# Eighteen seven-product units in the FFN's down projection, with their weight sums made ahead and kept in HBM

## The chip, the core and the metric

The kernel runs on one core of one Trainium2 chip. The metric is the device time of one execution in microseconds (us). Five engines with their own instruction streams share the work: TensorE (PE in the profile, its weight loads PEld), VectorE (DVE), ScalarE (ACT), GpSimd (POOL) and SyncE (SP). SP only starts DMA transfers, and POOL mostly does so here. Each engine takes its instructions in order and waits at the first one whose inputs or buffer are not ready.

## What is computed

One layer of a decoder trunk in float32: 256 tokens, D = 2048, feed-forward width 5632. The part that matters is the feed-forward network (FFN) behind the mixer, which has the two attention branches (MLA, 16 heads; a sliding window), their gates and `w_out`:

```python
def conv_ffn(h, w_up, conv_w, conv_b, w_down):
    a, b = jnp.split(h @ w_up, 2, axis=-1)
    ap = jnp.pad(a, ((0, 0), (CONV_WIDTH - 1, 0), (0, 0)))
    c = conv_b
    for j in range(CONV_WIDTH):
        c = c + conv_w[j] * ap[:, j:j + S]
    return (jax.nn.gelu(c, approximate=True) * b) @ w_down

def reference(...):
    for l in range(DEPTH):
        h = rms_norm(x, norm_mix_pre[l])
        y = hybrid_mixer(h, ...)
        x = x + rms_norm(y, norm_mix_post[l])
        h = rms_norm(x, norm_ffn_pre[l])
        y = conv_ffn(h, ffn_w_up[l], ffn_conv_w[l], ffn_conv_b[l], ffn_w_down[l])
        x = x + rms_norm(y, norm_ffn_post[l])
    return x
```

Each weight is read from HBM once; with everything else the profile counts 277.79 MB read.

## The kernel before

**A product in three passes.** Every float32 operand is split into a high part `hi` and a rest `lo`. A product of two tiles is hi·hi + hi·lo + lo·hi (`mm3`, L174–177): three 128x128 by 128x512 matmuls, at L175, L176 and L177. The split of a weight tile is `convert` (L133–145): ScalarE copies the raw tile into `whi` (L143), VectorE subtracts it from the raw tile into `wlo` (L144). A raw tile is 128 x 1024 floats, 512 KB, loaded by the SP queue (`wchunk`, or `raw_row` at L147–152). There is a ring of three raw tiles and a ring of four hi/lo pairs; a "flex" place makes it five raws or five pairs, by the stage.

**Down projection.** `w_down` has 44 rows of tiles (k = 0 to 43, each 128 x 2048). FFN columns come in eleven groups c of four k each: `ffn_up` (L1185–1222) makes up and gate columns, `conv_cols` (L1077–1092) does the convolution, the GELU and the gate product on 128x256 tiles, and the result stands as hi/lo tiles for the down projection. After c = 0 to 5 follows **down A**: k = 0 to 23 for all 2048 output columns, as two column pairs p = 0, 1 of 1024 each. After c = 6 to 10 follows the rest: **down B** for k = 24 to 43 and columns 0 to 1023, then plain products (`down`, j = 2, 3) for columns 1024 to 2047.

**Units.** `pair_gemm` (L205) works on two rows of k at a time, so on a 2 x 2 block product: two token halves, two k, two column halves. A plain unit, "p" in the order strings, takes 8 tile products, 24 matmuls. A seven-product unit, "s", gets by with 7 (21 matmuls) by a scheme of Strassen's kind. It needs sums of the activation tiles (`token_sums`, L278–288: `g_sums` and `b_sums`, made on VectorE during the up projection) and sums of the weight tiles. `seven` (L224–250) makes the latter on the spot: POOL's queue loads the two rows as `even` and `odd` (L227, L228), VectorE makes two tiles of sums `ta`, `tb` with four 128x512 subtracts (L232–235), and `odd`, half of `even`, `ta` and `tb` are converted: 3.5 raw tiles against a plain unit's two. The orders are `PAIR_ORDER = ("psppsppsppsp", "ppsppsppsppp")` for down A (4 + 3 units "s") and `B_ORDER = "pppsppspsp"` for down B (3): 10 units "s" and 24 "p".

**What sets the order.** `tick()` counts steps (one per weight tile of k in a product), and `at(t, f)` hangs work on step t: each `tick` emits what hangs on it. A scheduler then sorts what was written, engine by engine. The MLA units (attention of 16 heads) hang on steps of the products of the gates and of the sliding-window branch's output (`out_b`, `gate_b`), so that they run between their matmuls.

Of the kernel before, what the change touches and what calls it, by code (L numbers as in the profile page):

```python
# [11 lines left out]
F32 = mybir.dt.float32  # L12
# [25 lines left out]
SC_MLA = (128 + 64) ** -0.5  # L38
GELU_C = math.sqrt(2.0 / math.pi)


def trunk_layer(ctx, tc, x, x_cols_in, conv_cols_in, g_mix_post, g_ffn_post, w_in, w_q, w_kv,
# [103 lines left out]

    def raw_row(src):  # L147
        i = cnt[0]
        cnt[0] += 1
        raw = ring_tile("raw", f"raw{i}", F32, in_turn("raw"))  # L150
        nc.sync.dma_start(raw, src)
        return raw
# [51 lines left out]

    def pair_gemm(name, w, k0, c0, order, act_of, s_of, kind, d, place, sums):  # L205

        c11, c12, c21, c22 = c = banks(kind, f"c{name}_")
        q, used = [], set()
        row = lambda k: w[(k0 + k) * P:(k0 + k + 1) * P, c0:c0 + 1024]
        half = lambda w_, i: tuple(x[:, i * 512:(i + 1) * 512] for x in w_)  # L210

        def mul(o, x, w_, last=False):
            mm3(o, *x, *w_, id(o) not in used, last)
            used.add(id(o))

        def plain(u, last):
            for k in (2 * u, 2 * u + 1):
# [4 lines left out]
                tick()  # L222

        def seven(u, last):  # L224
# [5 lines left out]
            lo_, hi_ = slice(0, 512), slice(512, 1024)  # L230
            w_ = convert(odd, 1024)
            vec.tensor_tensor(ta[:, lo_], even[:, hi_], even[:, lo_], op=ALU.subtract)  # L232
            vec.tensor_tensor(ta[:, hi_], odd[:, hi_], even[:, hi_], op=ALU.subtract)
            vec.tensor_tensor(tb[:, lo_], odd[:, hi_], ta[:, lo_], op=ALU.subtract)
            vec.tensor_tensor(tb[:, hi_], odd[:, lo_], tb[:, lo_], op=ALU.subtract)
# [12 lines left out]
            mul(q6, s2, half(w_, 0), last)  # L248
            mul(c21, act_of(2 * u + 1, 1), half(w_, 1))
            tick()  # L250
            if last:
                d0, d1, d2, d3 = d() if callable(d) else d

                def first_sums():
                    act.copy(d0, q1)
                    vec.tensor_tensor(d1, d0, q6, op=ALU.add)
                    vec.tensor_tensor(d2, d1, q7, op=ALU.add)

                def more_sums():
                    vec.tensor_tensor(d3, d2, q5, op=ALU.add)  # L260
                    vec.tensor_tensor(d1, d1, q5, op=ALU.add)

                at(now[0], first_sums)
                at(now[0] + 1, more_sums)

        n = order.count("s")
        plain_of, seven_of = iter(range(n, len(order))), iter(range(n))
        for i, kd_ in enumerate(order):
            if kd_ == "s":
                u = next(seven_of)  # L270
                seven(u, u == n - 1)
            else:
                plain(next(plain_of), i == len(order) - 1)
        return c
# [464 lines left out]
    out_b(0, tb[0], (pss, "s"))  # L739
    tb[1], tb[2] = gate_pair(1)  # L740
    esg.close()

# [143 lines left out]

    b = now[0] + 26
    for u in range(8):
# [3 lines left out]

    for j in range(1, 4):
        out_b(j, tb[j], (pss, "s") if j == 1 else None)
        if j == 1:
            tb[3] = gate_b(3)
    at_ = [slot("b", p) for p in range(8)]
# [180 lines left out]
    def conv_cols(k, a, b, slot):  # L1078
# [6 lines left out]
        vec.scalar_tensor_tensor(cc[:, 2:256], a[:, 0:254], w0, cc[:, 2:256], op0=ALU.mult, op1=ALU.add)  # L1085
        act.activation(uu, cc, AF.Square)
        vec.tensor_scalar(uu, uu, 0.044715, 1.0, op0=ALU.mult, op1=ALU.add)
        vec.tensor_tensor(uu, uu, cc, op=ALU.mult)
        act.activation(uu, uu, AF.Tanh, scale=GELU_C)
# [78 lines left out]
    s_tiles = []  # L1168

    def g_sums(u):  # L1170

        if u % 2 == 0:
            s_tiles.append(sb(p3, [P, D], f"s_{u // 2}", F32R, tag=f"x2_{u // 2}"))
# [44 lines left out]

    es7 = ffn_up0()
    for c in range(1, 6):  # L1220
        if c == 2:
            for i in range(8):
                at(now[0] + i, lambda i=i: park(i // 4, i % 4))
        if c == 4:
            for u in range(4):
                at(now[0] + 3 + 3 * u, lambda u=u: g_sums(u))
        ffn_up(c, 4 * c)

# [4 lines left out]

    sevens_done = [0]

    def down_place():
        sevens_done[0] += 1
        i = sevens_done[0]
        if i % 2:
            both = sb(p6, [P, D], f"rr{i}", tag="gp")  # L1240
            return both[:, 0:1024], both[:, 1024:2048]
        return [sb(p6, [P, 1024], f"rr{i}{n}", tag="f" + n, bufs=2) for n in "ab"]

    def f_sums():
        return [sb(p6, [P, 1024], f"t{n}{cnt[0]}", tag="f" + n, bufs=2) for n in "ab"]

    for p in range(2):
        d = [dsum[t][2 * p + j] for t in range(NT) for j in range(2)]
        c = pair_gemm(f"d{p}", w_down, 0, 1024 * p, PAIR_ORDER[p], lambda k, t: (GH(k)[:, t * P:(t + 1) * P], GL(k)[:, t * P:(t + 1) * P]),
                      lambda u: s_of[u], p, d, down_place, f_sums)  # L1250
        for n_, (o, x_) in enumerate(zip(d, c)):
            at(now[0] + n_, lambda o=o, x_=x_: vec.tensor_tensor(o, o, x_, op=ALU.add))
    gpost2 = sb(p6, [P, D], "gpost2", tag="gp")
    pool.dma_start(gpost2, g_ffn_post.partition_broadcast(P))
    sb_tiles = []
    sb_of = {}

    def b_sums(u):

        if u % 2 == 0:  # L1260
            sb_tiles.append(sb(p3, [P, D], f"sb_{u // 2}", F32R, tag=f"x2_{u // 2}"))
        hi, lo = (sb_tiles[u // 2][:, (u % 2) * 1024 + i * 512:(u % 2) * 1024 + (i + 1) * 512] for i in range(2))
        a, m = (sb(s_pool[0], [P, 512], f"sb{n}{u}", tag="hx", bufs=2) for n in "am")
        sb_of[u] = token_sums(gtiles[u].bitcast(F32), a, m, hi, lo)

    for c in range(6, 11):
        if c == 9:
            for u in range(B_ORDER.count("s")):
                at(now[0] + 10 + 4 * u, lambda u=u: b_sums(u))
        ffn_up(c, 4 * (c - 6))  # L1270
# [3 lines left out]
    def z_block(acc, b, t):  # L1274
# [6 lines left out]
        act.activation(jt[:, :n], z, AF.Square, accum_out=ssz[t][:, b:b + 1])  # L1281
        vec.tensor_tensor(zo, z, gpost2[:, c0:c0 + n], op=ALU.mult)

# [24 lines left out]

    b_done = [0]

    def a_tiles(i, *n):
        return [sb(base, [P, 1024], f"dt{i}_{k}", tag=f"ahl{k}") for k in n]

    def b_place():
        b_done[0] += 1
        return a_tiles(b_done[0], *((0, 1) if b_done[0] % 2 else (4, 5)))

    ud = []

    def ud_tiles():  # L1320
        ud[:] = [x_[:, j * 512:(j + 1) * 512] for x_ in a_tiles(9, 4, 5) for j in range(2)]
# [7 lines left out]
    c_db = pair_gemm("db", w_down, 24, 0, B_ORDER, lambda k, t: (GH(k)[:, t * P:(t + 1) * P], GL(k)[:, t * P:(t + 1) * P]),  # L1329
                     lambda u: sb_of[u], 0, ud_tiles, b_place, lambda: a_tiles(20 + b_done[0], *((2, 3) if b_done[0] % 2 else (6, 7))))  # L1330
    for i in range(4):
# [110 lines left out]
```

## Time and profile before

| what | us |
|---|---|
| median of three runs | 1466.92 (1466.32 to 1467.46) |
| the profiled execution, its own time | 1466.82 |
| its span in the profile | 1464.7 |

From the trace, the stages that the change touches, by their first and last matmul:

| stage | us from the span's start |
|---|---|
| `out_b(1)`, `gate_b(3)`, `out_b(2)` begin | 283.8 |
| first MLA unit | 357.1 |
| FFN group c = 0, its second half | 754.8 to 776.4 |
| c = 1 | 776.4 to 822.9 |
| c = 2 to 5 | 822.9 to 1000.9 |
| down A, both column pairs | 1000.9 to 1126.8 |
| c = 6 to 10 | 1126.8 to 1349.4 |
| down B, columns 0 to 1023 | 1349.4 to 1402.3 |
| down, j = 2 and 3 | 1402.3 to 1456.9 |

The profile is read like this. A row of groups names line, engine, operation, output and inputs, shapes and count; behind it the busy time in all, the mean in ns of one, and the engine's idle time ahead of them with what ended it. The windows view gives one row per stretch: its length, then for each engine busy time and number of instructions, then the granted TensorE clock (1.00 is full speed), the busy share of the 16 DMA engines and the rate in GB/s. The waits view gives, per engine, line and releaser, the sum in us, the count and the longest.

### The profile page before, as it was taken

To read this page: it belongs to the slowest core of one execution; us is meant where nothing else is said; L and a number is where in the kernel's file an instruction comes from. 1 tells how busy PE (TensorE), PEld (TensorE's weight loads), DVE (VectorE), ACT (ScalarE), POOL (GpSimd) and SP (SyncE) were. 2 spreads that over 40 slices of the span, in tenths; PEclk is the share of its full clock that TensorE was granted. 3 is DMA by queue.
4 is the path that set the end of the run, shared out by engine and by line. 5 is a ranking of instruction groups with operands and counts; after the bars stand their busy time and mean duration, and the time that the engine had idled before them with its cause. 6 is when DMAs were issued, how large, how long until landed. Compare 5 with 4: busy or idle time off the path is not lost.

```text
span 1464.7 us, 20974 instructions
## 1 busy us (share of the span) xinstructions
PE 1454.3 (99%) x7567; PEld 1242.8 (85%) x7567; DVE 1088.9 (74%) x1925; ACT 837.7 (57%) x1382; POOL 70.2 (5%) x123
## 2 busy tenths in 40 slices
PE   9999999999999999999999999999999999999997
PEld 7888888888888888888888888888888888888886
DVE  7788896645667665768799976778786687677776
ACT  7588874544555554445666655555454565565553
POOL 0012110000000001000000000000000000000000
PEclk9999999999999999999999999999999999999999
DMA  8755376477655559755766666665656666667573
GB/s 296 216 164 168 105 261 197 160 212 199 188 159 159 165 162 337 263 186 173 235 206 179 199 188 187 191 187 185 206 192 207 201 186 191 186 196 232 163 234 136
DMA packets 147605, 287.60 MB, mean 196 GB/s; under 512 B 18428, under 2 KB 29597, under 8 KB 147373
## 3 DMA queue, kind: packets, MB, share of 16 engines
q1 hardware_dynamic: 137824, 252.60, 56.2%
q0 software_dynamic: 9584, 33.61, 7.3%
q8 instruction: 59, 0.97, 0.3%
q14 instruction: 46, 0.37, 0.1%
q10 hardware_dynamic: 92, 0.05, 0.0%
HBM read 277.79 MB, written 8.44 MB: 195 GB/s over the span
## 4 chain that ended last, share of the span: by engine, by line
PE 94%; DVE 2%; issue 2%; ACT 1%; DMA 1%; POOL 0%; DVEq 0%; ACTq 0%; POOLq 0%
PE accg L175 12%; PE accg L177 12%; PE accg L176 12%; PE ua L1185 10%; PE ub L1185 10%; PE ua L1189 5%; PE ub L1189 5%; PE cd L177 2%; PE cd L175 2%; PE cd L176 2%; PE mpo L875 1%; PE cg L175 1%; PE cw L177 1%; PE cg L177 1%; PE cw L176 1%
## 5 line engine op out<-in xcount | busy, mean ns | idle before, releaser
L144 DVE TENSOR_TENSOR wlo<-raw,whi 128x1024 fp32r<-128x1024 f32 (+2 forms) x470 | 568.4, 1214 | 248.2 <-ACT whi L143 241.2
L143 ACT CAST whi<-raw 128x1024 fp32r<-128x1024 f32 (+2 forms) x470 | 487.9, 1043 | 405.0 <-PE accg L177 156.9
L175 PE MATMUL accg<-whi,ahl 128*128 128x512 f32 (+1 forms) x416 | 162.8, 391 | 0.0
L177 PE MATMUL accg<-whi,ahl 128*128 128x512 f32 (+1 forms) x416 | 160.6, 386 | 0.0
L176 PE MATMUL accg<-wlo,ahl 128*128 128x512 f32 (+1 forms) x416 | 159.8, 384 | 0.0
L1185 PE MATMUL ub<-ahl,whi 128*128 128x512 f32 x640 | 154.6, 391 | 0.0
L1185 PE MATMUL ua<-ahl,whi 128*128 128x512 f32 x640 | 154.6, 391 | 0.0
L175 PE MATMUL accg<-whi,bhl 128*128 128x512 f32 x378 | 148.1, 392 | 0.0
L177 PE MATMUL accg<-whi,bhl 128*128 128x512 f32 x378 | 147.4, 390 | 0.0
L176 PE MATMUL accg<-wlo,bhl 128*128 128x512 f32 x378 | 147.3, 390 | 0.0
L1185 PEld LDWEIGHTS ub<-ahl,whi 128*128 128x128 f32 x640 | 117.5, 188 | 22.9 <-ACT cc L1083 0.3
L1185 PEld LDWEIGHTS ua<-ahl,whi 128*128 128x128 f32 x640 | 117.5, 188 | 22.7
L177 PEld LDWEIGHTS accg<-whi,ahl 128*128 128x128 f32 x416 | 78.1, 188 | 15.4
L176 PEld LDWEIGHTS accg<-wlo,ahl 128*128 128x128 f32 x416 | 78.2, 188 | 13.1
L175 PEld LDWEIGHTS accg<-whi,ahl 128*128 128x128 f32 x416 | 78.2, 188 | 13.0
L1189 PEld LDWEIGHTS ub<-ahl,wlo 128*128 128x128 f32 x640 | 82.2, 191 | 3.2
L1189 PEld LDWEIGHTS ua<-ahl,wlo 128*128 128x128 f32 x640 | 82.2, 191 | 3.1
L1189 PE MATMUL ua<-ahl,wlo 128*128 128x256 f32 x640 | 83.7, 283 | 0.0
L177 PEld LDWEIGHTS accg<-whi,bhl 128*128 128x128 f32 x378 | 71.0, 188 | 14.8
L175 PEld LDWEIGHTS accg<-whi,bhl 128*128 128x128 f32 x378 | 71.0, 188 | 14.4
L1189 PE MATMUL ub<-ahl,wlo 128*128 128x256 f32 x640 | 83.2, 283 | 0.0
L176 PEld LDWEIGHTS accg<-wlo,bhl 128*128 128x128 f32 x378 | 71.0, 188 | 14.3
(616 smaller groups left out, 2376.7 us busy)
## 6 DMA issues: line engine op xcount, KB each, us to landing
raw<-in_ffn_w_up_dram SPq DMA_DIRECT2D x176, 512.0 KB, 4.5
raw<-in_w_in_dram SPq DMA_DIRECT2D x105, 512.0 KB, 4.5
raw<-in_ffn_w_down_dram SPq DMA_DIRECT2D x68, 512.0 KB, 4.6
raw<-in_w_o_swa_dram SPq DMA_DIRECT2D x32, 512.0 KB, 4.0
raw<-in_w_o_mla_dram SPq DMA_DIRECT2D x32, 512.0 KB, 5.4
raw<-in_w_out_dram SPq DMA_DIRECT2D x26, 512.0 KB, 4.5
bias<-strip POOLq DMA_DIRECT2D x16, 256.0 KB, 4.3
raw<-in_mla_w_q_up_dram SPq DMA_DIRECT2D x32, 128.0 KB, 2.5
```

What stands on the lines that cost most here:

```text
L143: act.copy(hi[:, a:b], raw[:, a:b])
L144: vec.tensor_tensor(lo[:, a:b], raw[:, a:b], hi[:, a:b].bitcast(F32), op=ALU.subtract)
L175: pe.matmul(o, ah, bh, start=start, stop=False)
L176: pe.matmul(o, ah, bl, start=False, stop=False)
L177: pe.matmul(o, al, bh, start=False, stop=stop)
L875: pe.matmul(o, w(t), p_[:, c], start=n == 0, stop=n == 5)
L1185: pe.matmul(acc[i], hi[:, c], hn[p][:, j * 512:(j + 1) * 512], start=p + j == 0, stop=stop)
L1189: pe.matmul(acc[i][:, 0:256], lo[:, c], hn[p][:, j * 512:j * 512 + 256], start=False, stop=False)
```

## The change

- Eight more units become seven-product units: `PAIR_ORDER` has 6 + 6 "s" and `B_ORDER` 6. That is 18 "s" and 16 "p".
- The weight sums of all 18 are made ahead. `park_sums` hangs on steps of other stages: POOL loads the two rows (1 MB) into a staging tile, VectorE makes the four 128x512 subtracts in place (`less`, tied in written order by `keep_in_program_order`), POOL writes the two tiles of sums to HBM. Four are made during `out_b(1)`, `gate_b(3)` and `out_b(2)` (five steps apart), eight in c = 1 to 4 (seven or eight steps apart), six in c = 6 to 8 (eight steps apart).
- `seven_parked` takes the place of `seven`: SP's queue loads the odd row, half of the even row and the two tiles of sums, 3.5 raw tiles, and each is converted. No subtracts are left there.
- In down A and down B the ring of raw tiles is seven deep: the three, and tiles that are free in these stages (`fa`, `fb`; in B the halves of `ahl`, which hold the up projection's activations until c = 10 ends). In down A the flex place goes from raws to hi/lo pairs at step 8.
- Token sums are made for 6 units (used by both pairs) and 6, before 4 and 3.
- The GELU's polynomial folds 0.044715 into the scale of the Square: one VectorE instruction in place of two, for 44 column tiles.
- `out_b(1)`, `gate_b(3)` and `out_b(2)` are written ahead of the MLA units, which begin two steps after them; the matmuls come out in the order of before. The norm's gain `gpost2` is loaded into other tiles before down B.

```diff
+    def park_sums(name, w, k, c0, pl, tag, t0, bufs=None):
+
+        td = [dram.tile([P, 1024], F32, name=f"{name}{i}") for i in range(2)]
+        st = []
+
+        def load():
+            st.append(sb(pl, [P, D], f"{name}s", tag=tag, bufs=bufs))
+            for i in range(2):
+                pool.dma_start(st[0][:, i * 1024:(i + 1) * 1024], w[(k + i) * P:(k + i + 1) * P, c0:c0 + 1024])
+
+        def less(o, x, y):
+            o, x, y = (st[0][:, i * 512:(i + 1) * 512] for i in (o, x, y))
+            tc.keep_in_program_order(vec.tensor_tensor(o, x, y, op=ALU.subtract))
+
+        def even():
+            less(0, 1, 0)
+            less(1, 3, 1)
+            pool.dma_start(td[0], st[0][:, 0:1024])
+
+        def odd():
+            less(3, 3, 0)
+            less(2, 2, 3)
+            pool.dma_start(td[1], st[0][:, 1024:2048])
+
+        at(t0 - 5, load)
+        at(t0, even)
+        at(t0 + 1, odd)
+        return td
...
+        def seven_parked(u, last):
+            s1, s2, s3, s4 = s_of(u)
...
+            w_ = convert(raw_row(row(2 * u + 1)), 1024)
+            mul(c11, act_of(2 * u + 1, 0), half(w_, 0))
+            mul(c12, s4, half(w_, 1))
+            w_ = convert(raw_row(row(2 * u)[:, 0:512], 512), 512)
+            mul(q1, act_of(2 * u, 0), half(w_, 0), last)
+            w_ = convert(raw_row(parked[u][0]), 1024)
+            mul(q5, s1, half(w_, 0), last)
+            mul(q7, s3, half(w_, 1), last)
+            tick()
+            w_ = convert(raw_row(parked[u][1]), 1024)
+            mul(q6, s2, half(w_, 1), last)
+            mul(c21, act_of(2 * u + 1, 1), half(w_, 0))
+            tick()
...
+    parked_a = [park_a(i, pg, "gr", now[0] + 5 + 5 * i, bufs=2) for i in range(EARLY)]
+    out_b(1, tb[1], (pss, "s"))
+    tb[3] = gate_b(3)
+    out_b(2, tb[2])
...
-    b = now[0] + 26
+    b = now[0] + 2
...
-        act.activation(uu, cc, AF.Square)
-        vec.tensor_scalar(uu, uu, 0.044715, 1.0, op0=ALU.mult, op1=ALU.add)
-        vec.tensor_tensor(uu, uu, cc, op=ALU.mult)
+        act.activation(uu, cc, AF.Square, scale=GELU_R)
+        vec.scalar_tensor_tensor(uu, uu, 1.0, cc, op0=ALU.add, op1=ALU.mult)
...
+    for i in range(2 * NA - EARLY):
+        parked_a.append(park_a(i + EARLY, p6, "gp", now[0] + 8 + 15 * i // 2))
...
+    f_raw = lambda n: lambda name: sb(p6, [P, 1024], name, tag="f" + n, bufs=2)
+
+    def deep_raws():
+        turn_flex("w")
+        more_raw[:] = [raw_of, f_raw("a"), raw_of, f_raw("b"), raw_of, f_raw("a"), f_raw("b")]
+
+    turn_flex("raw")
+    at(now[0] + 8, deep_raws)
...
+    parked_b = [park_sums(f"tb{i}_", w_down, 24 + 2 * i, 0, p6, "gp", now[0] + 6 + 8 * i) for i in range(NB_)]
...
+    a_raw = lambda k: lambda name: a_tile(name, k)
+    more_raw[:] = [raw_of, a_raw(2), raw_of, a_raw(3), raw_of, a_raw(6), a_raw(7)]
...
-B_ORDER = "pppsppspsp"
+B_ORDER = "psspsspssp"
-PAIR_ORDER = ("psppsppsppsp", "ppsppsppsppp")
+PAIR_ORDER = ("ppspspsspssp", "ppspspsspssp")
+EARLY = 4
```

Three places show how instructions move. The first is VectorE in down A, around one "s" unit of the second column pair (`rr` is its pair of raw rows, loaded by POOL; `ta`, `tb` the sums). Before:

```order
L232 TENSOR_TENSOR ta746_10892<-rr7_10889 128x512
L233 TENSOR_TENSOR ta746_10892<-rr7_10889 128x512
L234 TENSOR_TENSOR tb746_10893<-rr7_10889,ta746_10892 128x512
L144 TENSOR_TENSOR wlo736_10798<-ta734_10774,whi736_10797 128x1024
L235 TENSOR_TENSOR tb746_10893<-rr7_10889,tb746_10893 128x512
L144 TENSOR_TENSOR wlo737_10808<-tb734_10775,whi737_10807 128x1024
L144 TENSOR_TENSOR wlo739_10820<-raw738_10817,whi739_10819 128x1024
L144 TENSOR_TENSOR wlo741_10838<-raw740_10835,whi741_10837 128x1024
```

After, the last two "s" units and the "p" behind them, in the same stage:

```order
L145 TENSOR_TENSOR wlo791_11082<-raw790_11079,whi791_11081 128x1024
L145 TENSOR_TENSOR wlo793_11094<-raw792_11091,whi793_11093 128x512
L145 TENSOR_TENSOR wlo795_11103<-raw794_11100,whi795_11102 128x1024
L145 TENSOR_TENSOR wlo797_11115<-raw796_11112,whi797_11114 128x1024
L145 TENSOR_TENSOR wlo799_11127<-raw798_11124,whi799_11126 128x1024
L145 TENSOR_TENSOR wlo801_11139<-raw800_11136,whi801_11138 128x512
L145 TENSOR_TENSOR wlo803_11148<-raw802_11145,whi803_11147 128x1024
L145 TENSOR_TENSOR wlo805_11160<-raw804_11157,whi805_11159 128x1024
L145 TENSOR_TENSOR wlo807_11172<-raw806_11169,whi807_11171 128x1024
L145 TENSOR_TENSOR wlo809_11193<-raw808_11190,whi809_11192 128x1024
```

The subtracts are gone from the stage, and "s" units stand back to back.

The second place is VectorE in c = 2, among the conversions of up-projection weights and the GELU of that group (`uu`, `cc`). Before:

```order
L144 TENSOR_TENSOR wlo567_8651<-raw566_8648,whi567_8650 128x1024
L1090 SCALAR_TENSOR_TENSOR uu8_8750<-uu8_8750,cc8_8749 128x256
L1087 TENSOR_SCALAR uu9_8807<-uu9_8807 128x256
L1087 TENSOR_SCALAR uu10_8864<-uu10_8864 128x256
L1088 TENSOR_TENSOR uu9_8807<-uu9_8807,cc9_8806 128x256
L144 TENSOR_TENSOR wlo569_8673<-raw568_8670,whi569_8672 128x1024
```

After (`ta7_s` is the staging tile of one pair of rows):

```order
L145 TENSOR_TENSOR wlo567_8733<-raw566_8730,whi567_8732 128x1024
L233 TENSOR_TENSOR ta7_s_8639<-ta7_s_8639 128x512
L145 TENSOR_TENSOR wlo569_8758<-raw568_8755,whi569_8757 128x1024
L233 TENSOR_TENSOR ta7_s_8639<-ta7_s_8639 128x512
L1159 SCALAR_TENSOR_TENSOR uu8_8841<-uu8_8841,cc8_8840 128x256
L233 TENSOR_TENSOR ta7_s_8639<-ta7_s_8639 128x512
L1157 SCALAR_TENSOR_TENSOR uu9_8897<-uu9_8897,cc9_8896 128x256
L233 TENSOR_TENSOR ta7_s_8639<-ta7_s_8639 128x512
L1157 SCALAR_TENSOR_TENSOR uu10_8953<-uu10_8953,cc10_8952 128x256
L145 TENSOR_TENSOR wlo571_8796<-raw570_8793,whi571_8795 128x1024
```

The four subtracts of one pair of rows now stand among the conversions, and the GELU has one instruction (L1157) where it had two (L1087, L1088).

The third place is SP's queue where down B begins. Before, it loads the rows of the first three plain units (the "s" units' rows are POOL's):

```order
L131 DMA raw920_13150<-in_ffn_w_up_dram 128x2x512
L151 DMA raw922_13190<-in_ffn_w_down_dram 128x1024
L151 DMA raw924_13208<-in_ffn_w_down_dram 128x1024
L151 DMA raw926_13239<-in_ffn_w_down_dram 128x1024
L151 DMA raw928_13257<-in_ffn_w_down_dram 128x1024
L151 DMA raw930_13288<-in_ffn_w_down_dram 128x1024
L151 DMA raw932_13306<-in_ffn_w_down_dram 128x1024
```

After (`tb0_0` and `tb0_1` are the first unit's two tiles of sums, `tb1_0` and `tb1_1` the second's; the raws' numbers, as in raw970, rise in the order in which the conversions take them):

```order
L132 DMA raw968_13388<-in_ffn_w_up_dram 128x2x512
L160 DMA raw970_13432<-in_ffn_w_down_dram 128x1024
L160 DMA raw974_13484<-in_ffn_w_down_dram 128x1024
L160 DMA raw972_13450<-in_ffn_w_down_dram 128x1024
L160 DMA raw978_13505<-tb0_0_11210 128x1024
L160 DMA raw976_13496<-in_ffn_w_down_dram 128x512
L160 DMA raw984_13553<-in_ffn_w_down_dram 128x512
L160 DMA raw986_13562<-tb1_0_11212 128x1024
L160 DMA raw988_13574<-tb1_1_11213 128x1024
L160 DMA raw980_13517<-tb0_1_11211 128x1024
L160 DMA raw990_13598<-in_ffn_w_down_dram 128x1024
L160 DMA raw982_13541<-in_ffn_w_down_dram 128x1024
```

The queue now carries all rows of two "s" units at the start, and issues some ahead of others that are used sooner: `tb0_1_11211`, the first unit's second tile of sums, stands behind three tiles of the next unit.

More of the change, by code (lines that the diff above doesn't have):

```diff
@@ L39 @@
 GELU_C = math.sqrt(2.0 / math.pi)
+GELU_R = math.sqrt(0.044715)
 def trunk_layer(ctx, tc, x, x_cols_in, conv_cols_in, g_mix_post, g_ffn_post, w_in, w_q, w_kv,
@@ L145, in convert, with raw_row @@
         return hi, lo
-    def raw_row(src):
+    more_raw = []
+    raw_of = lambda name: ring_tile("raw", name, F32, False)
+    def raw_row(src, n=1024):
         i = cnt[0]
         cnt[0] += 1
-        raw = ring_tile("raw", f"raw{i}", F32, in_turn("raw"))
-        nc.sync.dma_start(raw, src)
+        if more_raw:
+            make = more_raw.pop(0)
+            more_raw.append(make)
+            raw = make(f"raw{i}")
+        else:
+            raw = ring_tile("raw", f"raw{i}", F32, in_turn("raw"))
+        nc.sync.dma_start(raw[:, :n], src)
         return raw
@@ L203, in banks, with weight_sums, park_a, pair_gemm @@
                 for i in range(4)]
-    def pair_gemm(name, w, k0, c0, order, act_of, s_of, kind, d, place, sums):
+    def weight_sums(even, odd, ta, tb):
+        a, b = slice(0, 512), slice(512, 1024)
+        vec.tensor_tensor(ta[:, a], even[:, b], even[:, a], op=ALU.subtract)
+        vec.tensor_tensor(ta[:, b], odd[:, b], even[:, b], op=ALU.subtract)
+        vec.tensor_tensor(tb[:, a], odd[:, b], ta[:, a], op=ALU.subtract)
+        vec.tensor_tensor(tb[:, b], odd[:, a], tb[:, a], op=ALU.subtract)
+    def park_sums(name, w, k, c0, pl, tag, t0, bufs=None):
[20 more added lines that the diff above has]
+        return td
+    def park_a(i, pl, tag, t0, **kw):
+        return park_sums(f"ta{i}_", w_down, 2 * (i % NA), 1024 * (i // NA), pl, tag, t0, **kw)
+    def pair_gemm(name, w, k0, c0, order, act_of, s_of, kind, d, place=None, sums=None, parked=None):
         c11, c12, c21, c22 = c = banks(kind, f"c{name}_")
@@ L222, in plain @@
                 tick()
+        def seven_parked(u, last):
+            s1, s2, s3, s4 = s_of(u)
+            if not q:
+                q[:] = banks(1 - kind, f"q{name}_")
+            q1, q5, q7, q6 = q
+            w_ = convert(raw_row(row(2 * u + 1)), 1024)
[11 more added lines that the diff above has]
+            tick()
+            if last:
+                end_sums()
         def seven(u, last):
@@ L229, in seven @@
             ta, tb = sums()
-            lo_, hi_ = slice(0, 512), slice(512, 1024)
             w_ = convert(odd, 1024)
[L232 to L235, printed above, removed]
+            weight_sums(even, odd, ta, tb)
             if not q:
@@ L251, in seven, with end_sums, first_sums, more_sums @@
             if last:
[L252 to L264, printed above, removed]
+                end_sums()
+        def end_sums():
+            q1, q5, q7, q6 = q
+            d0, d1, d2, d3 = d() if callable(d) else d
+            def first_sums():
+                act.copy(d0, q1)
+                vec.tensor_tensor(d1, d0, q6, op=ALU.add)
+                vec.tensor_tensor(d2, d1, q7, op=ALU.add)
+            def more_sums():
+                vec.tensor_tensor(d3, d2, q5, op=ALU.add)
+                vec.tensor_tensor(d1, d1, q5, op=ALU.add)
+            at(now[0], first_sums)
+            at(now[0] + 1, more_sums)
         n = order.count("s")
@@ L270, in pair_gemm @@
                 u = next(seven_of)
-                seven(u, u == n - 1)
+                (seven_parked if parked else seven)(u, u == n - 1)
             else:
@@ L891, in trunk_layer @@
         mla_unit(u, b + 4 * u)
[L893 to L896, printed above, removed]
+    out_b(3, tb[3])
     at_ = [slot("b", p) for p in range(8)]
@@ L1226, in trunk_layer @@
                 at(now[0] + 3 + 3 * u, lambda u=u: g_sums(u))
+        if c == 5:
+            for u in range(4, NA):
+                at(now[0] + 3 + 5 * (u - 4), lambda u=u: g_sums(u))
         ffn_up(c, 4 * c)
@@ L1232, in down, with turn_flex @@
         return gemm(xh, xl, w_down, k0, nk, c0, n, split=split, ps=ps)
[L1234 to L1245, printed above, removed]
+    def turn_flex(kind):
+        flex[0] = kind
+        turn.update(raw=0, w=0)
+    f_raw = lambda n: lambda name: sb(p6, [P, 1024], name, tag="f" + n, bufs=2)
[4 more added lines that the diff above has]
+    at(now[0] + 8, deep_raws)
     for p in range(2):
@@ L1264, in b_sums @@
         sb_of[u] = token_sums(gtiles[u].bitcast(F32), a, m, hi, lo)
+    parked_b = [park_sums(f"tb{i}_", w_down, 24 + 2 * i, 0, p6, "gp", now[0] + 6 + 8 * i) for i in range(NB_)]
     for c in range(6, 11):
         if c == 9:
-            for u in range(B_ORDER.count("s")):
-                at(now[0] + 10 + 4 * u, lambda u=u: b_sums(u))
+            for u in range(NB_):
+                at(now[0] + 2 + 4 * u, lambda u=u: b_sums(u))
         ffn_up(c, 4 * (c - 6))
```

32 lines of the change are left out of this document (18 added, 14 removed).

## The prediction

> **What bounds the kernel now.** I read the page first, busy times and the chain of waits, then the waits view of PE.
>
> ```profile
> span 1464.7 us, 20974 instructions
> PE 1454.3 (99%) x7567; PEld 1242.8 (85%) x7567; DVE 1088.9 (74%) x1925; ACT 837.7 (57%) x1382; POOL 70.2 (5%) x123
> ...
> PE 94%; DVE 2%; issue 2%; ACT 1%; DMA 1%; POOL 0%; DVEq 0%; ACTq 0%; POOLq 0%
> PE warm L77 <- DVE ramp L66: 1.1, 1, 1.1
> PE pstrip L349 <- DMA sel<-in_strip_sel_dram: 0.8, 1, 0.8
> PE cdb L176 <- DVE wlo L144: 0.2, 1, 0.2
> ```
>
> PE is busy 99% of the span and makes 94% of the chain that ended last. In the whole execution the view shows three PE waits, two at the start and one of 0.2 us in down B. So the time is the number of matmuls times their pitch, as long as weights arrive converted. Whether they do is asked stage by stage, with the windows view (length; busy time and count for PE, PEld, DVE, ACT, POOL; clock; DMA share; GB/s):
>
> ```profile
> 283.80:349.40 65.60, 65.60 (x291) 54.30 (x291) 34.16 (x33) 29.32 (x31) 1.10 (x2) 1.00 0.72 210
> 571.00:584.00 13.00, 13.00 (x63) 10.77 (x62) 9.26 (x15) 5.84 (x7) 1.63 (x4) 1.00 1.04 383
> 776.40:822.90 46.50, 46.50 (x274) 41.04 (x273) 42.35 (x82) 30.73 (x54) 0.00 (x0) 1.00 0.61 186
> 822.90:1000.90 178.00, 178.00 (x1025) 157.32 (x1024) 131.42 (x224) 101.36 (x163) 0.54 (x1) 1.00 0.64 190
> 1000.90:1126.80 125.90, 125.90 (x557) 104.28 (x556) 97.17 (x114) 64.20 (x73) 6.33 (x12) 1.00 0.61 196
> 1126.80:1349.40 222.60, 222.60 (x1282) 196.73 (x1281) 164.56 (x272) 124.23 (x195) 2.11 (x4) 1.00 0.67 199
> 1349.40:1402.30 52.90, 52.74 (x233) 43.38 (x232) 39.65 (x53) 27.41 (x36) 1.06 (x2) 1.00 0.55 174
> ```
>
> Down A (1000.9) runs without a gap. Seven "s" and seventeen "p" are 7 x 21 + 17 x 24 = 555 matmuls (the row has two of the neighbouring groups besides), so the pitch is 125.9 / 555 = 0.2268 us. The clock is full throughout. A step of the up projection is 222.6 / 80 = 2.78 us, one of a plain product 12 x 0.2268 = 2.72.
>
> **What it removes.** Five units in down A and three in down B turn from "p" to "s": 8 x 3 = 24 matmuls, 24 x 0.2268 = **5.44 us** off the path. No other matmul is added or goes. The whole question is what feeds them.
>
> **Conversions in the down stages.** The groups by shape give the prices:
>
> ```profile
> L144 DVE TENSOR_TENSOR wlo<-raw,whi 128x1024 fp32r<-128x1024 f32 x458 | 558.7, 1224 | 246.2 <-ACT whi L143 239.3 <-PE ub L1185 3.0 <-PE ua L1185 2.5
> L144 DVE TENSOR_TENSOR wlo<-raw,whi 128x512 fp32r<-128x512 f32 x4 | 2.6, 690 | 2.0 <-ACT whi L143 2.0
> L143 ACT CAST whi<-raw 128x1024 fp32r<-128x1024 f32 x458 | 479.8, 1052 | 402.3 <-PE accg L177 156.2 <-PE ua L1185 48.7 <-DMA raw<-in_ffn_w_down_dram 48.1
> L143 ACT CAST whi<-raw 128x512 fp32r<-128x512 f32 x4 | 2.4, 616 | 1.9 <-DMA raw<-in_w_in_dram 1.9
> L232 DVE TENSOR_TENSOR ta<-rr 128x512 f32<-128x512 f32 x4 | 2.8, 688 | 0.1
> L284 DVE TENSOR_TENSOR sm<-sa,sm 128x128 f32<-128x128 f32 x4 | 1.2, 288 | 0.1
> L1087 DVE TENSOR_SCALAR uu<-uu 128x256 f32<-128x256 f32 x44 | 12.2, 287 | 0.7 <-ACT uu L1086 0.5
> L1088 DVE TENSOR_TENSOR uu<-uu,cc 128x256 f32<-128x256 f32 x44 | 18.3, 419 | 0.3
> L1207 DVE SCALAR_TENSOR_TENSOR f<-ub,f 128x256 f32<-128x256 f32 x40 | 14.2, 417 | 10.4 <-ACT f L1206 10.4
> ```
>
> An "s" costs PE 21 x 0.2268 = 4.76 us. Before, VectorE gave it 3 x 1.224 + 0.69 = 4.36 for conversions and 4 x 0.688 = 2.75 for sums: 7.11, more than PE, so the kernel could afford few of them, with "p" (2.45 on VectorE, 5.44 on PE) between. After, the 2.75 are gone and even "ss" fits: 4.36 against 4.76 on VectorE, 3 x 1.052 + 0.616 = 3.77 on ScalarE. VectorE no longer limits these stages, and the one stall of down B, where a `wlo` came late, may go with the sums:
>
> ```profile
> 1370.46 0.39 PE L175 MATMUL cdb<-whi,bhl 128*128 128x512 f32 x1
> ...
> 1371.00 0.50 PE L176 MATMUL cdb<-wlo,bhl 128*128 128x512 f32 x1 [0.15 <-DVE wlo L144]
> ```
>
> Start to start that is 0.54 us where the pitch is 0.23, and this matmul takes 0.11 longer than the one ahead: some 0.4 us, a gain between 0 and 0.4. I take 0.4, against a loss below.
>
> **Sums that move.** 18 x 2.75 = 49.5 us of VectorE work, 27.5 of it there before, go to stages where PE sets the pace. Token sums (two at about 0.69 and four at 0.288, 2.5 us for a unit) come five times more, 12.7 us; the GELU pays it back, (0.287 + 0.419 - 0.417) x 44 = 12.7 us. By stage: in 283.8 to 349.4 VectorE is busy 34.16 of 65.6, and four parks add 11. In c = 1 it is 42.35 of 46.5, two parks add 5.5, the GELU takes off 1.2: 46.7, full. In c = 2 to 5, 131.42 + 16.5 + 5.1 - 4.6 = 148 of 178. In c = 6 to 10, 164.56 + 16.5 + 7.6 - 5.8 = 183 of 222.6. So only c = 1 is over, by 0.2 us, and there conversions run ahead. ScalarE's waits in c = 1 to 5 show it:
>
> ```profile
> ACT whi L143 <- PE ua L1185: 22.6, 17, 2.7
> ACT whi L143 <- PE ub L1185: 20.1, 19, 2.7
> ```
>
> ScalarE waited 42.7 us for PE to give back a pair, that is with every pair full, four of them at 2.78 us. This hides the sums; I cost them at nothing. Without that cover c = 1 would cost 0.2 us, and every park up to its 2.75.
>
> **Park traffic.** A park loads 1.05 MB and writes 1.05 MB. In c = 1 to 4 that is 2.1 MB in 7.5 steps (20.9 us), 100 GB/s on top of 190; in the early stage 2.1 MB in 5 steps (13.6 us), 154 on top of 210: 364 GB/s for 55 us. Both are under the 383 GB/s that the stretch at 571 shows with PE full. The load is issued five steps (13.6 us) ahead of its subtracts. If it is later, the subtract holds VectorE's queue, so the `wlo` behind it, and PE only after four pairs (11 us) more. Cost nothing; bound from above in the rivals.
>
> **Loads of the down stages.** This is the one place where the sum could turn. An "s" now moves 3.5 x 0.524 = 1.835 MB where it moved 1.05. "ss" needs 3.67 MB in 9.53 us, 385 GB/s; "ssp" 4.72 in 14.97, 315; down A and B together 18 x 1.835 + 16 x 1.049 = 49.8 MB in 762 x 0.2268 = 172.8 us, 288 GB/s, where the rows show 196 and 174. The nearest rows:
>
> ```profile
> raw<-in_ffn_w_down_dram SPq DMA_DIRECT2D x68, 512.0 KB, 4.6
> raw<-in_w_o_mla_dram SPq DMA_DIRECT2D x5, 512.0 KB, 6.9
> ACT whi L143 <- DMA raw<-in_ffn_w_down_dram: 25.2, 9, 6.3
> ```
>
> The second is from the stretch 571 to 584, the densest loading, with PE full. A place of the seven-deep ring comes back after two units, 9.5 us in "ss", less 2.3 us of conversion: 7.2 us for a landing that took 4.6 at 190 GB/s and 6.9 at 383. It fits, narrowly. The third row is down A before: ScalarE waited nine times for a load, without PE noticing. Where down B begins it is tighter. The second unit's odd row stands in SP's queue behind a place that the fourth pair of conversions gives back, so it starts some 1.7 us into B at best (0.616 + 0.69 for the half row's conversion, which begins as B does, and an estimated 0.4 until the issue); it must be there at 5.44 + 4.76 - 2.28 = 7.9. At 4.6 it is 1.6 early, at 6.9 it is 0.7 late. Bounds for each of the seven "ss" (four in A, three in B): 0 and 0.7. I take 0.5 in all, near the lower end, since six of the seven begin with a ring filled during the "p" ahead.
>
> [...]
>
> **The sum.** 1466.82 (the profiled execution) - 5.44 - 0.4 + 0.5 = 1461.5. That execution lies 0.1 below the median 1466.92, so against the median it is the same within rounding. Forecast **1461.5**, its own range 1460.6 to 1462.4.
>
> **Rivals.** *A. Loads become the bound; slower.* If the down stages get less than 49.8 MB / 178.3 us = 279 GB/s (178.3 being 786 x 0.2268, what the same units take now), the gain is gone. At 265 GB/s they take 188 us, 15 more than planned, and the kernel 1476; at 270, 1473. For it: no stage of that length ran over 210 GB/s in the rows, the landing of 6.9 us at the dense place, and tiles that must be written to HBM and read again. Against it: 383 GB/s with nothing lost on PE. *B. The "ss" come late by up to 0.7 each*, in-order loads behind places that come back late: two to seven of them in place of the 0.5, 1462.4 to 1465.9, in the middle 1464.1. For it: the start of B above. Against it: "p" units between, which need only 193 GB/s. *C. Parks hold VectorE.* One staging tile serves all parks of the FFN stages, so a load waits for the last write. Write and load at 6.9 each behind the subtracts' two steps give 5.6 + 6.9 + 6.9 = 19.4 of 20.9 us. If each of the 18 lost 0.3 us, 5.4 are gone: 1466.9, no change. Against it: eleven microseconds of pairs ahead. That the matmuls don't go is no rival: PE's own list of instructions is 24 matmuls shorter.
>
> **How the numbers follow.** Forecast 0.66, B 0.18, C 0.05, A 0.11. A measurement of this kernel can tell about 0.2%, 2.9 us, from no change: faster is below 1464.0. Faster: 0.66 + two thirds of B + a fifth of C = 0.79. Same: the rest of B and most of C, and the lightest cases of A: 0.11. Slower: 0.10. The range takes the forecast's and nearly all of B, 1460.6 to 1466.0; A and half of C are left out, and the lowest tail.
>
> **What would show it.** In the changed profile, down A (540 matmuls) should last 122.5 us and down B (222) 50.4, PE gapless, at 280 to 320 GB/s. VectorE in down A falls to 12 x 4.36 + 12 x 2.45 plus what else is there, some 90 us. C = 1 keeps its 46.5. PE waits on `wlo` or on DMA in "ss" mean B; a rate stuck below 280 with ScalarE waiting for `raw` means A; PE waits in c = 1 to 8 or in 283 to 357 mean C. The forecast is wrong if the 24 matmuls are gone and the down stages are not 5.4 us shorter, or if a stage that only took in moved work gets longer.

## The result

| kernel | median, us | lowest to highest | runs |
|---|---|---|---|
| before | 1466.46 | 1465.82 to 1467.64 | 10 |
| changed | 1469.97 | 1467.43 to 1473.88 | 10 |

The ratio of the changed kernel to the one before is 1.0025, with a 95% interval of 1.0014 to 1.0035: slower by about 3.5 us, where 1461.5 was forecast. Its runs also spread over 6.5 us, those of before over 1.8. A fixed amount of extra work would add the same time to every run, so the spread suggests that something in it is near a limit.

The page of the changed kernel, from the lines on span, busy time and the chain that ended last:

```profile
span 1470.6 us, 21276 instructions
PE 1453.6 (99%) x7543; PEld 1239.7 (84%) x7543; DVE 1119.9 (76%) x1959; ACT 850.3 (58%) x1403; POOL 98.6 (7%) x176
...
PE 75%; DVE 10%; DMA 9%; ACT 3%; issue 2%; DVEq 0%; ACTq 0%; SPq 0%
```

The 24 matmuls are gone (7543 against 7567). But PE makes 75% of the chain instead of 94%, and VectorE and DMA have come in with 10% and 9%. The waits view of PE, which had one entry of 0.2 us behind the start:

```profile
PE ub L1261 <- DVE wlo L145: 4.0, 4, 2.3
PE ua L1261 <- DVE wlo L145: 1.5, 2, 1.2
PE qd L184 <- ACT whi L144: 1.1, 1, 1.1
...
PE qd L185 <- DVE wlo L145: 0.8, 1, 0.8
PE cd L185 <- DVE wlo L145: 0.3, 1, 0.3
```

Most of it waits in `ub` and `ua`, the up projection, whose matmuls the change does not touch. The windows view places it (columns as in the prediction):

```profile
283.80:349.40 65.60, 65.60 (x291) 54.35 (x290) 44.28 (x49) 29.37 (x31) 7.51 (x14) 1.00 0.92 304
776.30:889.40 113.10, 113.10 (x657) 100.07 (x656) 98.35 (x176) 65.62 (x109) 9.61 (x18) 1.00 0.77 248
889.40:1006.40 117.00, 112.62 (x642) 98.74 (x642) 88.44 (x145) 63.44 (x104) 6.40 (x12) 1.00 0.78 251
1006.40:1133.50 127.10, 124.96 (x542) 102.27 (x541) 92.33 (x100) 74.52 (x85) 1.06 (x2) 0.99 0.82 276
1133.50:1357.80 224.30, 223.24 (x1281) 196.96 (x1280) 176.68 (x292) 126.30 (x200) 12.80 (x24) 1.00 0.78 251
1357.80:1408.30 50.50, 50.50 (x224) 41.81 (x223) 41.54 (x51) 31.75 (x40) 0.00 (x0) 1.00 0.92 321
```

| stage | before | changed | difference |
|---|---|---|---|
| c = 1 to 5 | 224.5 | 230.1 | +5.6 |
| down A | 125.9 | 127.1 | +1.2 (122.5 forecast) |
| c = 6 to 10 | 222.6 | 224.3 | +1.7 |
| down B | 52.9 | 50.5 | -2.4 (50.4 forecast) |

These add up to +6.1; the two spans differ by 5.9. Down B did what was forecast, at 321 GB/s and without a gap. The loss is in the up projection, where parks came in, and where down A starts behind it. The first park stage (283.8), where the flex place belongs to raws, runs at 304 GB/s without a gap. The second half of c = 1 to 5 loses; the first half (776.3 to 889.4) does not.

Why, ScalarE's waits in c = 1 to 5 (776.4 to 1000.9) of the changed kernel tell:

```profile
ACT whi L144 <- DMA raw<-in_ffn_w_up_dram: 53.7, 30, 6.2
```

The DMA view of the same stretch (count, size, median us from issue to landing):

```profile
raw<-in_ffn_w_up_dram SPq DMA_DIRECT2D x74, 512.0 KB, 4.8
ta<-ta_s POOLq DMA_DIRECT2D x16, 512.0 KB, 4.7
ta_s<-in_ffn_w_down_dram POOLq DMA_DIRECT2D x14, 512.0 KB, 6.6
```

Before, ScalarE waited 42.7 us there for PE to give back a pair: the converter was ahead. Now it waits 53.7 us for raw tiles: it is behind. Yet the raws' median landing only rose to 4.8 us; the same row of the kernel before:

```profile
raw<-in_ffn_w_up_dram SPq DMA_DIRECT2D x74, 512.0 KB, 4.4
```

The worst place, from the changed kernel's timeline of ScalarE (start, duration, in brackets the idle time ahead and what ended it):

```profile
942.62 1.07 ACT L144 CAST whi<-raw 128x1024 fp32r<-128x1024 f32 x1
943.56 0.62 ACT L1153 ACTIVATE cc<-f,cvT 128x256 f32<-128x256 f32 x1
950.41 1.04 ACT L144 CAST whi<-raw 128x1024 fp32r<-128x1024 f32 x1 [6.23 <-DMA raw<-in_ffn_w_up_dram]
```

And of PE:

```profile
952.77 1.22 PE L1261 MATMUL ub<-ahl,wlo 128*128 128x256 f32 x8 [2.25 <-DVE wlo L145]
```

A raw tile was issued at 940.4, behind a park's 1 MB at 939.8, and landed 9.95 us later. ScalarE stood 6.2 us, and PE ran out of pairs. In the first half of the stage ScalarE stood 22.6 us for raw tiles as well (14 times, the longest 4.2), and PE did not wait at all: there the lateness was paid out of the stock of converted pairs.

### The profile page after: what moved, and what is told of

Read it like the earlier page. It is cut to its first block, busy times and chain, and to the rows that moved or that the text cites. A ratio compares the mean times of both kernels' runs of the same rounds, so it can differ in the third digit from the quotient of the medians.

```text
span 1470.6 us, 21276 instructions
## 1 busy us (share of the span) xinstructions
PE 1453.6 (99%) x7543; PEld 1239.7 (84%) x7543; DVE 1119.9 (76%) x1959; ACT 850.3 (58%) x1403; POOL 98.6 (7%) x176
## 4 chain that ended last, share of the span: by engine, by line
PE 75%; DVE 10%; DMA 9%; ACT 3%; issue 2%; DVEq 0%; ACTq 0%; SPq 0%
PE accg L184 12%; PE accg L186 12%; PE accg L185 12%; DMA raw<-in_ffn_w_up_dram 8%; PE ua L1257 4%; DVE wlo L145 4%; PE ub L1257 3%; PE ua L1261 2%; PE cd L185 2%; PE cd L186 2%; PE cd L184 2%; ACT whi L144 2%; PE ub L1261 2%; DVE ta_s L233 1%; PE mpo L948 1%
## 5 line engine op out<-in xcount | busy, mean ns | idle before, releaser
L145 DVE TENSOR_TENSOR wlo<-raw,whi 128x1024 fp32r<-128x1024 f32 (+2 forms) x526 | 624.5, 1195 | 243.0 <-ACT whi L144 238.0
L144 ACT CAST whi<-raw 128x1024 fp32r<-128x1024 f32 (+2 forms) x526 | 537.0, 1028 | 431.0 <-PE accg L186 157.3
L1257 PEld LDWEIGHTS ub<-ahl,whi 128*128 128x128 f32 x640 | 117.5, 188 | 22.6
```

The lines of the kernel that those rows point to most:

```text
L144: act.copy(hi[:, a:b], raw[:, a:b])
L145: vec.tensor_tensor(lo[:, a:b], raw[:, a:b], hi[:, a:b].bitcast(F32), op=ALU.subtract)
L1257: pe.matmul(acc[i], hi[:, c], hn[p][:, j * 512:(j + 1) * 512], start=p + j == 0, stop=stop)
```

## The experiments

Theory 1 after this view: the parks' transfers make the raw loads of the up projection late. There are three raw tiles, so one must come round (issue, landing, 1.05 + 1.22 us of conversion) within three steps, 8.3 us; a landing above 6.0 us puts the converter behind. Theory 2, the prediction's rival C: the parks' subtracts hold VectorE's in-order queue. Theory 3: the writes to HBM do it.

### No transfers, no subtracts, no writes

Each leaves out one part of the 14 parks in the FFN stages; the four early ones stay.

```diff
 e1_no_park_dma
+            if tag == "gp" and keep.get(name[:2]):
+                st.append(keep[name[:2]])
+                return
...
-            pool.dma_start(td[0], st[0][:, 0:1024])
+            if tag != "gp":
+                pool.dma_start(td[0], st[0][:, 0:1024])
 e2_no_park_sub
-            less(0, 1, 0)
-            less(1, 3, 1)
+            if tag != "gp":
+                less(0, 1, 0)
+                less(1, 3, 1)
 e3_no_park_write
-            pool.dma_start(td[0], st[0][:, 0:1024])
+            if tag != "gp":
+                pool.dma_start(td[0], st[0][:, 0:1024])
```

> The 14 parks of the FFN stages keep their four subtracts but neither load nor write (one load each in c = 1 and c = 6 fills the tile); the down stages read plain rows of w_down of the same size in place of their sums, so the output is not the reference's. Theory 1 (the parks' transfers make the up projection's raw loads late, in a ring of three, and the pairs ahead are used up): the 5.5 us lost in c = 3 to 5 and the 1.2 in c = 8 go, down A starts with its pairs ahead, 1461 to 1463. Theory 2 (the subtracts hold VectorE's queue): nothing gained, 1468 to 1472. Theory 3 (only the writes to HBM hurt): 1461 to 1463 as well.

> The 14 parks of the FFN stages keep loads and writes but not their subtracts, so raw rows are written and the output is not the reference's. Theory 1 (transfers): little gained, 1466 to 1471. Theory 2 (subtracts in VectorE's queue): the loss goes, 1461 to 1463. Theory 3 (writes): 1466 to 1471.

> The 14 parks of the FFN stages keep loads and subtracts but write nothing; the down stages read plain rows of w_down in place of those sums, so the output is not the reference's. Theory 1 (all transfers of the parks, the 1 MB load bursts above all): some of the loss stays, 1462 to 1467. Theory 2 (subtracts): 1468 to 1472. Theory 3 (writes alone): all of the loss goes, 1461 to 1463.

| kernel | median, us | lowest to highest | ratio to before, 95% |
|---|---|---|---|
| no transfers | 1460.58 | 1459.32 to 1461.92 | 0.9957 (0.9942 to 0.9972) |
| no subtracts | 1469.50 | 1467.77 to 1473.34 | 1.0024 (1.0012 to 1.0035) |
| no writes | 1465.45 | 1460.83 to 1469.14 | 0.9990 (0.9980 to 1.0001) |

Without the transfers the whole gain stands; without the subtracts nothing is gained. That speaks against theory 2. Alone it is not quite clean: without subtracts to wait for, the writes also start sooner after the loads. The five raws below keep every subtract, and settle it. Without the writes about half comes back in the median, so theory 3 falls too, as the only cause: loads and writes both count. Where PE loses the time differs between the profiled executions: without subtracts it waited in c = 1 already (at 794.0 and 810.4 us), without writes it waited in down A and in c = 6 to 10 (226.4 us there) and not in c = 1 to 5. The windows of the kernel without transfers, c = 1 to 5 and down A:

```profile
775.20:999.80 224.60, 224.60 (x1298) 198.62 (x1297) 188.37 (x322) 131.52 (x217) 0.00 (x0) 1.00 0.64 195
999.60:1122.20 122.60, 122.60 (x542) 101.52 (x541) 91.68 (x99) 73.36 (x83) 1.07 (x2) 1.00 0.81 270
```

VectorE has all of its added work there (188 us) and PE loses nothing. Down A, which still loads as many bytes, takes 122.6 us, the 122.5 of the forecast. So its excess in the changed kernel came with the stage ahead of it.

The kernel without subtracts still shows how a late load reaches PE. From its timeline in c = 1:

```profile
781.01 1.06 POOL L229 DMA_DIRECT2D ta_s<-in_ffn_w_down_dram  x2 [5.55 <-DMA ta<-ta_s]
...
782.07 11.16 SPq L132 DMA_DIRECT2D raw<-in_ffn_w_up_dram  x4
...
790.53 1.05 ACT L144 CAST whi<-raw 128x1024 fp32r<-128x1024 f32 x1 [2.66 <-DMA raw<-in_ffn_w_up_dram]
...
791.61 1.23 DVE L145 TENSOR_TENSOR wlo<-raw,whi 128x1024 fp32r<-128x1024 f32 x1 [3.28 <-ACT whi L144]
792.75 0.42 DVE L1161 SCALAR_TENSOR_TENSOR uu<-uu,cc 128x256 f32<-128x256 f32 x1
```

POOL starts two rows at 781.0. SP's raw at 782.07 lands at 790.45, after 8.4 us. ScalarE, then VectorE, stand in front of it, and the GELU's `uu` waits behind `wlo` in VectorE's queue. PE's waits view there names `uu`, not a load (3.1 us at `fT`). Followed back, it is the load: here a raw tile that took 8.4 us reached PE through VectorE's queue, and not as a missing pair.

### Five raws in the FFN stages

```diff
     es7 = ffn_up0()
+    flex[0] = "raw"
+    turn.update(raw=0, w=0)
...
     more_raw.clear()
-    turn.update(raw=0)
+    turn_flex("raw")
...
+    turn_flex("w")
     a_raw = lambda k: lambda name: a_tile(name, k)
```

> The whole change, with the two flex places given to raw tiles from c = 1 to 5 and c = 6 to 10: five raws and four hi/lo pairs where there were three and five. Theory 1 (late loads in a ring of three): a landing of up to 5 x 2.78 - 2.3 = 11.6 us is now covered where 6.0 was, so c = 1 to 5 lose 0 to 1 us and the time is 1461 to 1465. Theory 2 (subtracts hold VectorE): one pair less of cover, so the same or worse, 1470 to 1475. Theory 3 (writes): between them, 1462 to 1467.

1461.49 us (1460.73 to 1466.03), ratio 0.9971 (0.9961 to 0.9980). No transfer was taken away; two places were only renamed from pairs to raws. The profiled execution (1464.21) has one stall left, where down A goes over to c = 6:

```profile
1128.00:1131.40 3.40, 0.93 (x5) 0.51 (x4) 0.61 (x1) 1.41 (x2) 0.00 (x0) 1.00 0.10 38
1131.40:1134.00 2.60, 2.60 (x8) 2.02 (x7) 2.50 (x3) 2.57 (x3) 0.00 (x0) 0.51 0.30 47
```

At 38 GB/s hardly anything is loading: SP's queue had stood 2.6 us in front of a flex place that still held a pair of down A (it waited for a matmul of `cd`, the view of SP's waits says). The next experiment takes those out of use four steps earlier:

```diff
     for p in range(2):
...
+        if p:
+            at(now[0] + 20, lambda: turn_flex("raw"))
```

> The kernel e4_raw5 with one stall of its profile taken away: there SP's queue, at the start of c = 6, waited for flex places that still held hi/lo pairs of down A, and PE lost 4.2 us in the profiled execution (2.6 of stall, the rest at half clock behind it). Here the flex places are no longer given to pairs in the last four steps of down A. If that transition was what spread e4's times (1460.7 to 1466.0), the median is 1460.5 to 1461.5 and the spread under 3 us. If the spread comes from elsewhere (parks of c = 6 to 8), as e4: 1461 to 1462 with a spread of 5.

**1460.08 us** (1459.75 to 1460.42), ratio 0.9955 (0.9942 to 0.9969), beside 1466.47 for the kernel before. It beats both kernels, and its five runs spread over 0.7 us. ScalarE's waits in c = 1 to 5:

```profile
ACT whi L144 <- PE ua L1257: 24.0, 18, 2.7
ACT whi L144 <- PE ub L1257: 17.3, 14, 2.7
```

The raws' landing there, in the DMA view:

```profile
raw<-in_ffn_w_up_dram SPq DMA_DIRECT2D x73, 512.0 KB, 5.1
```

And the chain that ended last, from the page:

```profile
PE 96%; DVE 2%; ACT 1%; issue 1%; DMA 0%; DVEq 0%; ACTq 0%
```

The loads land later than in the changed kernel (median 5.1 against 4.8, and 14 of 74 took more than 6 us, the longest 9.0), at 263 GB/s against 250, with every subtract in its place. Yet ScalarE waits for PE again, as before, and PE has no wait in the stage. In this kernel late loads did no harm with enough of them under way: five raws cover 11.6 us, and the longest landing was 9.0.

### Fewer raws, or only in one part

> The kernel e5_raw5_tail with one raw tile fewer in the FFN stages: four raws and four pairs. Theory 1: a ring of four covers a landing of 4 x 2.78 - 2.3 = 8.8 us, above nearly all that the profiles show beside parks (90% under 6.7), so nearly all of the gain: 1460 to 1462. If it is something else that the fifth raw brings, between e5 and the changed kernel: 1463 to 1467.

```diff
+    deep = [2]
...
-        return flex[0] == kind and turn[kind] % (RAW + 2 if kind == "raw" else RING + 1) >= (RAW if kind == "raw" else RING)
+        return flex[0] == kind and turn[kind] % (RAW + deep[0] if kind == "raw" else RING + 1) >= (RAW if kind == "raw" else RING)
...
     flex[0] = "raw"
+    deep[0] = 1
```

1459.92 us (1459.29 to 1461.99), ratio 0.9958 (0.9943 to 0.9973): the fourth raw tile brings all of it, as 4 x 2.78 - 2.3 = 8.8 us says. In its trace 16 of 74 raws took more than 6 us, none more than 7.7, and PE has no wait. (The edit is not exactly a ring of four. Three of four loads find their place four steps back; the fourth goes to the flex place, which keeps its two buffers in turn, so it can start up to a step earlier.)

> The whole change with five raws in c = 1 to 5 alone; c = 6 to 10 keep three raws and five pairs. By theory 1 c = 6 to 8, where a park comes every 22 us, lose what the changed kernel lost there, 1 to 2 us, with some spread: 1461 to 1463. If three raws are enough at that spacing: as e5, 1460 to 1460.5.

```diff
     es7 = ffn_up0()
+    flex[0] = "raw"
+    turn.update(raw=0, w=0)
```

1462.56 us (1460.79 to 1465.39), ratio 0.9974 (0.9964 to 0.9983). Against 1460.08 that is some 2.5 us, at the upper end of what was expected and with its spread. The profiled execution (1462.92) puts only half of it where three raws are: c = 6 to 10 took 223.9 us, and 222.7 with five. PE's waits behind the start:

```profile
PE x2T L1071 <- DVE x L1068: 1.3, 1, 1.3
...
PE ub L1261 <- DVE wlo L145: 0.5, 1, 0.5
```

The second lies in c = 8. The first lies at 740.9 us, ahead of the FFN, in a place that this edit does not touch; what delayed it is not known. So three raws in c = 6 to 10 cost 1.2 us in this execution; how the other runs divide is open.

> The kernel before, with the two flex places given to raws in c = 1 to 5 and back to pairs in down A and after: a control for e4. Before has no stall there, so by theory 1 five raws give nothing: 1466 to 1467. If five raws and four pairs are better in themselves, whatever the parks do, it gains as e4 did, 1462 to 1464.

```diff
     es7 = ffn_up0()
+    flex[0] = "raw"
+    turn.update(raw=0, w=0)
     for c in range(1, 6):
...
+    flex[0] = "w"
+    turn.update(raw=0, w=0)
     for p in range(2):
```

1466.20 us (1465.04 to 1466.79), ratio 0.9997 (0.9988 to 1.0006). Five raws give nothing to the kernel before: the gain is not theirs.

### Are the bursts to blame?

```diff
-            for i in range(2):
+            for i in range(2 if tag != "gp" else 1):
                 pool.dma_start(st[0][:, i * 1024:(i + 1) * 1024], ...)
...
         at(t0 - 5, load)
+        if tag == "gp":
+            at(t0 - 3, lambda: pool.dma_start(st[0][:, 1024:2048], w[(k + 1) * P:(k + 2) * P, c0:c0 + 1024]))
```

> The whole change with three raws as it is, but each park of the FFN stages loads its two rows two steps (5.6 us) apart instead of at once; the same bytes in all. If the bursts do it (a raw load queued behind 1 MB lands 8 to 10 us late in a ring that covers 6), landings stay under 7 us and the loss of 5.5 us in c = 3 to 5 falls to 0 to 2: 1462 to 1466. If the bytes as such do it (the mean rate of 250 GB/s), no change: 1468 to 1472. If VectorE's queue waits for the later second row, worse: 1470 to 1474.

1469.27 us (1466.10 to 1471.63), ratio 1.0020 (1.0011 to 1.0029): nothing gained. I had taken the 1 MB burst for the culprit; spreading it by two steps leaves the median landing at 4.8 us and the time as it was. It did not make the landings punctual either: 13 of 68 raws took more than 6 us, the longest 10.4, where the unsplit loads had 12 of 67 and 9.95. So it is the added traffic on a ring of three; that no other spacing would help is not shown.

### The GELU

> The kernel e4_raw5 with the GELU of before (two VectorE instructions for one, 12.7 us more of VectorE over c = 0 to 10). If only late loads count, nothing is lost: 1461 to 1462.5. If VectorE's queue is near its limit beside the parks' subtracts, 1463 to 1468.

```diff
-        act.activation(uu, cc, AF.Square, scale=GELU_R)
-        vec.scalar_tensor_tensor(uu, uu, 1.0, cc, op0=ALU.add, op1=ALU.mult)
+        act.activation(uu, cc, AF.Square)
+        vec.tensor_scalar(uu, uu, 0.044715, 1.0, op0=ALU.mult, op1=ALU.add)
+        vec.tensor_tensor(uu, uu, cc, op=ALU.mult)
```

1462.50 us (1460.74 to 1464.77). This did not decide: `e4_raw5` itself spread up to 1466 through its stall at c = 6. The same edit on the clean kernel:

> The kernel e5_raw5_tail with the GELU of before: 12.7 us more of VectorE, nothing else. Theory 1 (only late loads in a short ring count): 1460 to 1461. If VectorE is near its limit beside the parks' subtracts: 1462 to 1464.

1459.83 us (1459.33 to 1460.75), ratio 0.9954 (0.9937 to 0.9970): 12.7 us more of VectorE cost nothing. The folded GELU is neither cause nor help.

## Why the prediction was wrong

**The gain itself was right.** With loads in time, down A takes 122.6 us and down B 50.5 (122.5 and 50.4 forecast), and the kernel 1460.08, 6.4 under before. The forecast's 5.44 + 0.4 make 5.8 of it (the spans of the two profiled executions differ by 6.0); the remaining half microsecond was not traced. The 0.5 us that the sum held back for the "ss" was not needed.

**The dense down stages were right.** They were the feared place, at up to 385 GB/s. Seven raws under way carry them: 276 GB/s in down A, 321 in down B, no wait of PE in B. Rivals A and B did not occur: the waits in down A fall in the first "s" behind two "p", not in an "ss", and with loads in time they are gone.

**The step that failed is "Park traffic", with its cost of nothing.** It set 100 GB/s on top of 190 against the 383 that the chip had shown, found room, and stopped. The room was there (250 GB/s came). What the parks cost measured +5.6 us in c = 1 to 5, +1.7 in c = 6 to 10, and 4.6 in down A (127.1 against 122.5), 11.9 in all against a gain of 5.8. The 383 GB/s had been reached with five raws; the FFN stages have three, since the flex place belongs to pairs there. With three, rate was not the limit (with five, the same stage moves 263 GB/s without a gap), but the time for one tile to come round: 4.4 + 2.3 = 6.7 of 8.3 us before, 1.6 to spare. Of the 67 raws issued between 776.4 and 1000.9 us whose landing the changed kernel's trace gives, 12 took more than 6 us; before, 2 of 69. For the seven-deep ring of the down stages the prediction had done this very sum (7.2 us for a landing of 4.6 to 6.9); at its own 6.9 a ring of three, with room for 6.0, is too short.

**The cover was there, but it was a stock.** The "eleven microseconds of pairs ahead" were true at c = 1, and in this execution they held for the first half of the stage. But a ring with 1.6 us to spare refills slowly, and the next park came before the stock was full again: ScalarE waited for PE to give back a pair, the sign of a full stock, 3.5 us in all of c = 1 to 5, where it had waited over 42 before. PE's first wait falls at 909.8 us; from there on late tiles reached PE. Down A then began with nothing ahead: its first "s", behind two "p", has PE's waits of 1.1 and 0.8 us, and part of its excess is the halved clock behind them (0.56 from 1023.0 to 1026.5 us, last section). That the whole 4.6 us came with the stage ahead is shown by the kernels whose raws came in time, which take 122.6.

**Rival C had the place and not the mechanism.** It named PE waits in c = 1 to 8, and the prediction's own sign of being wrong, a stage that only took in moved work getting longer, came too. But it put them on parks that hold VectorE's queue; the kernel without subtracts is as slow (1469.50), and the one with five raws keeps them all and loses nothing. VectorE's budget, on which much of the working went (46.7 of 46.5 us in c = 1, where 42.2 came), decided nothing.

**POOL's transfers delayed SP's.** In c = 1 to 5, SP's raws of `w_up` landed after 4.4 us in the median and 6.6 at worst before, and after 4.8 and 9.95 beside the parks; without the parks' transfers (`e1_no_park_dma`) the median is 4.4 again.

## What to carry to other kernels

When work with transfers is moved into a stage that looks idle, ask for each ring of that stage how long one tile takes to come round (issue, landing, conversion) against tiles in the ring times the step, not only how many GB/s are free. Here the stock of finished tiles covered the late loads up to 889.4 us (22.6 us of ScalarE's waits, none of PE's); against the series of parks the surplus of the ring counted, 1.6 us a round with three raws. And when a bandwidth is borrowed from another stage as proof of room, look at how many loads that stage had under way.

## What was not expected of the hardware

**The last part of a burst landed at a fifteenth of the rate.** At the worst stall, the DMA view of the changed kernel from 944 to 953 us (rate in 40 slices of 0.225 us):

```profile
GB/s 419 437 382 391 382 337 337 328 382 355 401 419 419 319 319 391 328 373 328 209 128 36 46 55 18 27 27 27 18 27 27 18 27 27 18 27 27 18 0 0
```

For the last 4 us the rate is some 25 GB/s, a fifteenth of the 373 from 944 to 948 us, and the busy share of the 16 DMA engines, the last but one number of the windows view, is 0.06 where it was 1.02:

```profile
950.00:952.00 2.00, 0.52 (x5) 0.31 (x3) 0.51 (x1) 1.58 (x3) 0.00 (x0) 1.00 0.06 25
```

The trace's packets run one at a time from 949.6 to 952.4, where 15 to 18 were under way from 944 to 948. The raw that ScalarE waited for landed in this tail, at 950.3. Why the last packets came one by one is not shown; the trace does not name a packet's engine. So this landing took 9.95 us, though at its end the DMA engines as a whole were nearly idle.

**Behind two stalls the granted clock was halved for 3.41 us; behind two others it was not.** In the changed kernel, behind PE's waits of 1.1 and 0.8 us:

```profile
1019.70:1022.50 2.80, 0.94 (x4) 0.24 (x2) 1.81 (x4) 2.71 (x4) 0.00 (x0) 1.00 0.54 154
1023.00:1026.50 3.50, 3.50 (x10) 2.71 (x9) 3.37 (x4) 2.63 (x4) 0.00 (x0) 0.56 0.98 372
```

The second row has ten matmuls in 3.5 us, where 15 fit: clock 0.56 granted. The trace's record of the granted clock has it at 0.50 for 3.41 us from 1023.42 us on, and at full speed ahead of it and behind. The rows of `e4_raw5` above show the same (0.51), and there the wait of 2.5 us cost 4.3: c = 6 to 10 took 227.0 us, and 222.7 in the kernel after it. But the wait of 2.25 us at 952.8 had no such tail, nor had one of 3.1 us in the kernel without subtracts (at 794.0): the clock stayed at 1.00.

What decides it is not shown. In the 3.4 us ahead of the two half-clock stretches PE was busy for 1.55 us (from 1020.01) and 0.93 us (`e4_raw5`, from 1128.0). At the two waits without a tail it was no busier: 1.15 us of the 3.4 from 949.4 us, and 0.90 us of the 4.0 from 790.0 us in the kernel without subtracts.
